# The second SwiGLU of each layer computed wholly in quads of seven products, with the output projection and the down projections reordered around its start

## The chip, the core and the metric

The kernel runs on one core of one Trainium2 chip. The metric is the device time of one execution in microseconds (us): 2252.36 us is the median of three runs of the kernel before (2252.14 to 2252.47).

The names of the engines are those of the profile: PE (matrix multiplication) with PEld (its weight loads), DVE (vector), ACT (scalar and activation), POOL and SP (here the queue that issues loads).

## The reference, cut to what matters

There are two layers (`DEPTH`), 512 positions (`SEQ`), a model width of 1024 and a hidden width of 2816 in each SwiGLU. A layer is

```
h = h + 0.5 * swiglu(rmsnorm(h, ffn1_norm), ffn1_w_gu, ffn1_w_down)
u = rmsnorm(h, mix_norm)                  # gated convolution and attention of u
h = h + merged @ w_o                      # output projection of the mixer
h = h + 0.5 * swiglu(rmsnorm(h, ffn2_norm), ffn2_w_gu, ffn2_w_down)
h = h + sigmoid(rmsnorm(h) @ w_pg) * (p @ w_pp)

swiglu(x): g, u = split(x @ w_gu);  return (silu(g) * u) @ w_down
```

The change concerns the line with `w_o` and the SwiGLU behind it, in both layers.

## The kernel before, in words

**Numbers in two parts.** The state `h` lies transposed in SBUF as eight tiles `h[0..7]` of 128 features by 512 positions. Every operand of a product is split into a rounded high part and a low part (`split`, `split_to`), and a product is the sum hi·hi + hi·lo + lo·hi, so three matrix multiplications (`mm3`, L266 to L270). Weights come from HBM as raw tiles `st` of 128x1024, which hold eight 128x128 blocks; ACT rounds a raw tile to `wh` (L71) and DVE subtracts to get `wl` (L72). There are four buffers each for `wh` and `wl` and ten for raw tiles, handed out in turn: the fifth split waits until PE has done with the first.

**A SwiGLU (`ffn`).** `normed` (L357) makes the split inputs `xs[k]` and the sum of squares of the eight `h[k]`; `rms` turns that sum into the factor `r`, which is applied behind the products. The 22 column blocks of the hidden width are computed in two ways. *Whole* blocks are plain projections: two column tiles (gate and up) times eight `xs`, 96 matrix multiplications of 512 columns for two blocks (`projs`, `proj`). *Quads* (`Sevens`, `Halved`) compute two blocks at once by seven products in place of eight: `Halved.row(j)` forms sums and differences of halves of `h[j]` and `h[j+4]` (`t`, `u`), and `Quad.part(j)` forms sums and differences of four raw weight tiles on DVE. Products 1, 2, 3, 4 and 6 are *joint*: eight wide multiplications of 512 columns (`wh` against high and low part together, L527) and eight narrow ones of 256 columns (`wl`, L533). Products 5 and 7 take 24 multiplications of 256 columns (L547). In `narrow_first` products the narrow ones come first.

**Accumulators of a quad.** Product 1 opens accumulator `b`; a copy of it by ACT (L552) opens `a`, which takes product 2; after product 6 another copy of `b` opens `d`, which takes 5 and 3; `b` goes on with 7 and 4. `Sevens.out` empties an accumulator: ACT copies one half (L556), DVE adds the other (L557), `finish` multiplies by `r`, applies silu and multiplies up with gate. PSUM holds two buffers for `b` (pool `bp`), one shared by `a` and `d` (pool `ap`), and two single banks (`mp`).

**Order.** The order on every engine comes from a scheduler that takes instructions by the order of the program and by its own estimate of when they are ready; `tc.issue_after(x)` adds that the instructions of the block that run on the engine of `x` stand behind `x` there. In `ffn`, all SwiGLUs but the very first begin with two whole blocks: `projs` of block 0 runs while DVE and ACT finish the norm and the rows, and the two projections of block 1 stand between the products of quad 1 (L727 to L741). From there on `next_quad` (L656) lays out every quad as product 1 of the next, product 4 of this one, a fill, 2, 6, a fill, 5, 7, 3, two fills. A *fill* (`fill`, L651) is a down projection `down(m, f0, f0+4)`: ACT writes 2·h[m] into a single bank (L640), 12 multiplications add four hidden blocks, and ACT writes half of the sum back to `h[m]` (L644).

**Output projection.** L1057 to L1060 compute `h[m] += w_o` block by block, m = 0 to 7.

Of the kernel before, what the change touches and what calls it, by code (L numbers as in the profile page):

```python
# [13 lines left out]
ALU = mybir.AluOpType  # L14
AX = mybir.AxisListType

P = 128
# [16 lines left out]
class Stream:  # L34
# [43 lines left out]
    def fill(self):  # L78
        return 0 if self.tiles is None else len(self.tiles) % 8
# [50 lines left out]
class Quad:  # L130


    def __init__(self, W, quarters):
        self.W = W
        for q in ("a11", "a21", "a22", "a12"):
            setattr(self, q, W.raw(quarters[q]))

    def part(self, j):

        W = self.W  # L140
        tt = W.nc.vector.tensor_tensor
        if j == 1:
# [16 lines left out]
        return W.split(self.a11)  # L159


class HiLo(tuple):
# [20 lines left out]
def trunk_kernel(ctx, tc, dims, x, p, positions, gains, rope_c, final_row, weights, out):  # L183
# [19 lines left out]
    class Banks:  # L203


        def __init__(self):
            self.scope, self.n = None, 0

        def close(self):
            if self.scope is not None:  # L210
                self.scope.close()
            self.scope = ExitStack()
            self.n += 1
# [8 lines left out]

        def paired(self):
            self.close()
            self.chain, self.seeded, self.single = self.pool("bp", 2), self.pool("ap", 1), self.pool("mp", 2)

    banks = Banks()
    ctx.callback(lambda: banks.scope.close())
# [4 lines left out]
    def two(pool, name):  # L233
        return pool.tile([P, 1024], F32, tag="bb", name=name).rearrange("p (w t) -> p w t", t=512)

    def PB(name):
        return two(banks.chain, name)

    def PA(name):
        return two(banks.seeded, name)  # L240

    def halves(t):
        return [t[:, 0, :], t[:, 1, :]]
# [9 lines left out]
    def split(src, name, scale=None, paired=False):  # L253
        v = X(name) if paired else (G(name + "h", F32R), G(name + "l", F32R))
        split_to(*v, src, scale)
        return v

    def split_to(hi, lo, src, scale=None):
        if scale is None:
            nc.scalar.copy(hi, src)  # L260
            return nc.vector.tensor_tensor(lo, src, hi.bitcast(F32), ALU.subtract)
# [54 lines left out]
    def gain(nm, l, k):  # L316
        c = col_at[nm, l] + k
        return cols[:, c:c + 1]
# [35 lines left out]
        nc.vector.scalar_tensor_tensor(r, t, 1.5 * scale, r, ALU.add, ALU.mult)  # L354
        return r

    def normed(nm, l, name, after=None, paired=True):  # L357

        xs, sq = [], Squares(name)
        for k in range(KD):  # L360
            xs.append(split(h[k], f"{name}x{k}", gain(nm, l, k), paired))
            sq.add(h[k])
            if after:
                after(k, xs)
        return xs, sq.parts()
# [81 lines left out]
    class Halved:  # L447
# [11 lines left out]
        def row(self, j, xs):  # L459

            self.own(j, xs)
            self.other(j, xs)

        def own(self, j, xs):

# [10 lines left out]
        def other(self, j, xs):  # L476

            H = S // 2
            left, right = slice(0, H), slice(H, S)
            k = j + KD // 2  # L480
            x, t, th, tl = self.half.pop(j)
            y, u = G(f"{self.name}y{j}"), G(f"{self.name}u{j}")
            nc.scalar.mul(y, h[k], gain(self.nm, self.l, k))
            nc.vector.tensor_tensor(t[:, right], y[:, right], x[:, right], ALU.subtract)
            nc.vector.tensor_tensor(u[:, left], t[:, right], x[:, left], ALU.add)
            nc.vector.tensor_tensor(u[:, right], y[:, left], u[:, left], ALU.subtract)
            split_to(th, tl, t)
            self.ys[7].append((th[:, right], tl[:, right]))
            for p_, at in ((2, left), (3, right)):
                self.ys[p_].append(self.both(xs[k], at))  # L490
            for p_, at in ((6, left), (4, right)):
                v = G(f"{self.name}u{j}_{p_}", F32R).rearrange("p (a t) -> p a t", t=H)
                split_to(v[:, 0, :], v[:, 1, :], u[:, at])
                self.ys[p_].append((v[:, 0, :], v))

    class Sevens:

# [6 lines left out]
        def __init__(self, w, l, name, ys, columns, done):  # L504
            self.w, self.l, self.name, self.ys, self.columns, self.done = w, l, name, ys, columns, done
            self.todo = {}
            self.narrow_first = ()

        def quad(self, n):
            if n not in self.todo:  # L510
# [9 lines left out]
        def joint(self, ps, d, j):  # L520

            hi, lo = d["w"].part(j)
            at = [slice(i * P, (i + 1) * P) for i in range(8)]
            def wide(last):
                for k, (_, pair) in enumerate(self.ys[j]):
                    for w in range(2):
                        nc.tensor.matmul(ps[:, w, :].rearrange("p (a t) -> p a t", t=self.H), hi[:, at[2 * k + w]], pair,  # L527
                                         start=j == 1 and k == 0, stop=last and k == 3, skip_group_check=True)

            def narrow(last):  # L530
                for k, (vh, _) in enumerate(self.ys[j]):
                    for w in range(2):
                        nc.tensor.matmul(ps[:, w, :self.H], lo[:, at[2 * k + w]], vh, start=False, stop=last and k == 3,  # L533
                                         skip_group_check=True)

            parts = (narrow, wide) if j in self.narrow_first else (wide, narrow)
            for i, part in enumerate(parts):
                part(i == 1)

        def product(self, ps, d, j):  # L540

# [6 lines left out]

        def seed(self, n, what):
            d = self.todo[n]  # L550
            d[what] = PA(f"{self.name}{n}{what}")
            nc.scalar.copy(d[what].rearrange("p w t -> p (w t)"), d["b"].rearrange("p w t -> p (w t)"))  # L552

        def out(self, n, ps, f, c):
            t = self.tile(n, f"o{f}{c}")
            nc.scalar.copy(t, ps[:, :, self.H:])  # L556
            nc.vector.tensor_tensor(t, ps[:, :, :self.H], t, ALU.add)  # L557
            self.done(n, f, c, t, t)

        def step(self, n, j):  # L560
            d, H = self.quad(n), self.H
# [23 lines left out]
                self.joint(d["b"], d, j)  # L585
                self.out(n, d.pop("b"), 1, 0)

    def ffn(l, nm, name, first=False, beside=iter(()), early=2):
# [26 lines left out]
        if not first:  # L615
            sevens.narrow_first = (3, 4, 6)

        def early_rows(k, xs):

            if 0 <= k - KD // 2 < early:  # L620
                ys.row(k - KD // 2, xs)

        xs, acc = normed(nm, l, name, early_rows)

        pss, pds = {}, {}

# [23 lines left out]

        def fill():  # L651
            if downs:
                m, f0 = downs.pop(0)
                down(m, f0, f0 + 4)

        def next_quad(n):  # L656

            for i, j in enumerate((1, 4, None, 2, 6, None, 5, 7, 3, None, None)):
                next(beside, None)
                if j is None:  # L660
                    if i < 9 or downs and downs[0][1] < f_last:
                        fill()
                    continue
                step(n if j == 4 else n + 1, j)
                if j == 6 and n % 2:
                    downs.extend((m, 2 * n - 2) for m in range(KD))

        cs = [[W.col(nm + "_w_gu", l, c + f * P, D) for c in (0, DFF)] for f in range(n_whole)]

# [7 lines left out]
        if first:  # L677
# [23 lines left out]
            downs.extend((m, 0) for m in range(KD))  # L701
            fill()
            with tc.issue_after(second):
                step(n0, 5)
# [1 line left out]
                step(n0, 3)  # L706
            sevens.narrow_first = (3, 4, 6)
            for _ in range(2):
                fill()
        else:  # L710
            pss[0] = whole(0)
# [12 lines left out]
            step(n0, 7)  # L724
            step(n0, 3)
        fill()
        for n in range(n0, np_ - 1):  # L727
            next_quad(n)

        f0 = f_last  # L730
        left = [m for m in range(KD) if (m, f0) in downs]
        assert len(left) == len(downs)
        spare = PA(f"{name}pd")[:, 0, :]
        for m in left[:3]:
# [23 lines left out]
    def mixer(l):  # L758
# [498 lines left out]
    for l in range(DEPTH):  # L1257
        ffn(l, "ffn1", f"a{l}", l == 0, rotary() if l == 0 else iter(()), 2 if l else 0)
        mixer(l)
        ffn(l, "ffn2", f"b{l}")  # L1260
        (ple_last if l == DEPTH - 1 else ple)(l)

    return W.halves
# [46 lines left out]
```

## Time and profile before

| | us |
|---|---|
| median of three runs | 2252.36 |
| the profiled execution's own time | 2252.33 |
| its span, first to last instruction | 2250.3 |
| PE busy in it | 2240.8 |
| DVE busy | 1743.5 |
| ACT busy | 1456.1 |
| POOL busy | 37.4 |

Busy time of PE counts overlapping multiplications once, and their ends are modelled, so what a stretch costs is read from the starts of its multiplications. The granted PE clock over the span is 0.999. In the first layer the output projection ends and the second SwiGLU begins at 729.15 us; tiles of that SwiGLU carry the prefix `b0`, those of the second layer `b1`.

### The profile page before, as it was taken

Reading aid. Unit: us, or ns where it says so; the run is one execution under the profiler, and the core shown is the slowest. Engines: PE = TensorE matmul, PEld = TensorE weight load, DVE = VectorE, ACT = ScalarE, POOL = GpSimd, SP = SyncE. Lnnn points to the kernel's source line nnn. Section 1 sums busy time; section 2 is a strip of 40 time slices with the busy share of each in tenths; the row PEclk is TensorE's granted clock in tenths of the full one; section 3 lists DMA queues with packets and bytes.
Section 4 is the critical chain, followed back from the end, with each engine's and each line's share of the span. In section 5 each row is a group of like instructions: output and inputs, shape, how many; then the busy total and the mean of one; then the engine's idle time right before and its main releaser. Section 6 shows DMA issues by size and latency. Waiting matters only on the chain.

```text
span 2250.3 us, 31142 instructions
## 1 busy us (share of the span) xinstructions
PE 2240.8 (100%) x12144; PEld 1947.7 (87%) x12144; DVE 1743.5 (77%) x2453; ACT 1456.1 (65%) x2246; POOL 37.4 (2%) x42
## 2 busy tenths in 40 slices
PE   9999999999999999999999999999999999999998
PEld 8888888888888888888888888888888888888887
DVE  8987768788866887776798777687889678777756
ACT  7666666576744666667676666764767357666664
POOL 0000000000200000000000000000001000000000
PEclk9999999999999999999999999999999999999999
DMA  5333332323132232334223233323222223333321
GB/s 215 99 113 104 103 122 75 112 76 104 47 104 84 94 103 97 107 107 141 75 94 104 96 106 108 113 88 102 92 76 75 94 75 103 104 104 103 108 99 38
DMA packets 63362, 223.04 MB, mean 99 GB/s; under 512 B 7280, under 2 KB 7280, under 8 KB 63216
## 3 DMA queue, kind: packets, MB, share of 16 engines
q1 hardware_dynamic: 62640, 220.28, 29.2%
q8 instruction: 95, 1.56, 0.3%
q10 hardware_dynamic: 576, 0.79, 0.1%
q14 instruction: 51, 0.42, 0.1%
HBM read 218.94 MB, written 2.10 MB: 98 GB/s over the span
## 4 chain that ended last, share of the span: by engine, by line
PE 97%; DVE 2%; ACT 1%; issue 0%; DVEq 0%
PE a0pd L268 2%; PE a1pd L268 2%; PE b0pd L268 2%; PE b1pd L268 2%; PE a0pd L269 2%; PE a0pd L270 2%; PE b1pd L269 2%; PE b0pd L269 2%; PE a1pd L269 2%; PE b1pd L270 2%; PE b0pd L270 2%; PE a1pd L270 2%; PE m0mop L268 1%; PE m1mop L269 1%; PE m0mop L269 1%; PE m1mop L270 1%
## 5 line engine op out<-in xcount | busy, mean ns | idle before, releaser
L72 DVE TENSOR_TENSOR wl<-st,wh 128x1024 fp32r<-128x1024 f32 (+1 forms) x508 | 614.7, 1212 | 227.5 <-ACT wh L71 224.1
L71 ACT CAST wh<-st 128x1024 fp32r<-128x1024 f32 (+1 forms) x507 | 527.9, 1044 | 306.6 <-PE m1Bp L269 13.9
L71 ACT CAST wh<-s 128x1024 fp32r<-128x1024 f32 x49 | 51.6, 1052 | 28.8 <-PE m1Cp L269 4.2
L72 DVE TENSOR_TENSOR wl<-s,wh 128x1024 fp32r<-128x1024 f32 x49 | 59.6, 1216 | 0.3 <-ACT wh L71 0.3
L152 DVE TENSOR_TENSOR st<-st,st 128x1024 f32<-128x1024 f32 x49 | 59.7, 1219 | 0.2
L154 DVE TENSOR_TENSOR s<-st,st 128x1024 f32<-128x1024 f32 x49 | 59.6, 1217 | 0.1
L149 DVE TENSOR_TENSOR st<-st,s 128x1024 f32<-128x1024 f32 x49 | 59.6, 1216 | 0.0
L157 DVE TENSOR_TENSOR st<-st,st 128x1024 f32<-128x1024 f32 x49 | 59.6, 1216 | 0.0
L644 ACT ACTIVATE h<-a0pd 128x512 f32<-128x512 f32 x40 | 23.7, 594 | 5.6 <-PE a0pd L270 5.3
L644 ACT ACTIVATE h<-b1pd 128x512 f32<-128x512 f32 x40 | 23.7, 592 | 4.9 <-PE b1pd L270 4.8
L644 ACT ACTIVATE h<-b0pd 128x512 f32<-128x512 f32 x40 | 23.7, 592 | 4.7 <-PE b0pd L270 4.6
L644 ACT ACTIVATE h<-a1pd 128x512 f32<-128x512 f32 x40 | 23.6, 591 | 4.5 <-PE a1pd L270 4.4
L640 ACT ACTIVATE a1pd<-h 128x512 f32<-128x512 f32 x40 | 24.0, 599 | 0.7
L640 ACT ACTIVATE b1pd<-h 128x512 f32<-128x512 f32 x40 | 23.9, 599 | 0.6
L640 ACT ACTIVATE b0pd<-h 128x512 f32<-128x512 f32 x40 | 23.9, 598 | 0.6
L640 ACT ACTIVATE a0pd<-h 128x512 f32<-128x512 f32 x40 | 23.9, 598 | 0.6
L107 POOL MEMSET wh<- 128x256 f32 x4 | 1.1, 314 | 1173.3 <-DVE wl L72 1173.3
L268 PE MATMUL a0p<-a0x,wh 128*128 128x512 f32 x44 | 17.1, 390 | 0.0
L269 PE MATMUL a0p<-a0x,wh 128*128 128x512 f32 x44 | 17.1, 390 | 0.0
L270 PE MATMUL a0p<-a0x,wl 128*128 128x512 f32 x44 | 17.1, 389 | 0.0
L263 ACT ACTIVATE b0x<-h,cols 128x512 fp32r<-128x512 f32 x8 | 5.8, 724 | 13.3 <-DVE h L1060 13.3
L263 ACT ACTIVATE b1x<-h,cols 128x512 fp32r<-128x512 f32 x8 | 5.8, 723 | 13.3 <-DVE h L1060 13.3
(6945 smaller groups left out, 7503.9 us busy)
## 6 DMA issues: line engine op xcount, KB each, us to landing
st<-in_weights SPq DMA_DIRECT2D x406, 512.0 KB, 3.3
h<-in_x SPq DMA_DIRECT2D x8, 256.0 KB, 5.4
st<-in_weights SPq DMA_DIRECT2D x7, 256.0 KB, 5.3
out<-e1d SPq DMA_DIRECT2D x4, 256.0 KB, 2.1
out<-fh SPq DMA_DIRECT2D x3, 256.0 KB, 2.2
e0pi<-in_p SPq DMA_DIRECT2D x2, 256.0 KB, 3.5
e1pi<-in_p SPq DMA_DIRECT2D x2, 256.0 KB, 3.8
fg<-in_final_row SPq DMA_DIRECT2D x2, 256.0 KB, 4.5
```

What stands on the lines that cost most here:

```text
L71: self.nc.scalar.copy(hi[:, w], src[:, w])
L72: self.nc.vector.tensor_tensor(lo[:, w], src[:, w], hi[:, w].bitcast(F32), ALU.subtract)
L149: tt(self.a12, self.a12, self.s, ALU.subtract)
L152: tt(self.a11, self.a11, self.a21, ALU.subtract)
L154: tt(self.s, self.a22, self.a11, ALU.subtract)
L157: tt(self.a21, self.a21, self.a22, ALU.add)
L263: nc.scalar.activation(hi, src, AF.Copy, scale=scale)
L268: nc.tensor.matmul(ps, wh, vh, start=first, stop=False, skip_group_check=seeded)
L269: nc.tensor.matmul(ps, wh, vl, start=False, stop=False, skip_group_check=seeded)
L270: return nc.tensor.matmul(ps, wl, vh, start=False, stop=last, skip_group_check=seeded)
L640: nc.scalar.mul(ps, h[m], 2.0)
L644: nc.scalar.mul(h[m], ps, 0.5)
```

## The change

In both second SwiGLUs (`quads=True`) there are no whole blocks left: the 22 hidden blocks are eleven quads, 0 to 10.

- The output projection computes blocks 0 and 4 together, k by k, in the two banks of the `ap` buffer, and then 1, 5, 2, 6, 3, 7; the norm follows that order. `own(j)` and `other(j)` of the rows are called as soon as `h[j]` and `h[j+4]` exist, so all four rows stand ahead of the first product.
- `Quad.early` splits parts 1 and 2 of quad 0 into ordinary 128x512 buffers and forms all sums of that quad's weights while the output projection runs.
- Product 1 of quad 1 and product 2 of quad 0 are computed in two parts: 1 of quad 0, wide part of 1 of quad 1, wide part of 2 of quad 0, 6 of quad 0, narrow part of 2, narrow part of 1; then 5, 7, 3, 4 of quad 0, 2 and 6 of quad 1, 1 of quad 2, and 5, 7, 3 of quad 1. The accumulator `d` of quad 0 has a PSUM buffer of its own (`PX`), which becomes the two single banks afterwards.
- The down projections start behind product 3 of quad 1, with blocks 0 and 1 alone for all m; blocks 2 and 3 follow, then four at a time. So each `h[m]` goes to PSUM and back once more. `fill` takes two of the short ones at a time, and also two where it meets `(0, f0, 4)`: in the first SwiGLUs of both layers the fills thus run one ahead.

```diff
+    def early(self, split):                                   # class Quad
+        tt = self.W.nc.vector.tensor_tensor
+        self.ready[1] = split(self.a11)
+        self.ready[2] = split(self.a12)
+        tt(self.a11, self.a11, self.a21, ALU.subtract)
+        self.s = self.W.buffer("s")
+        tt(self.s, self.a22, self.a11, ALU.subtract)
+        tt(self.a12, self.a12, self.s, ALU.subtract)
+        tt(self.a21, self.a21, self.a22, ALU.add)
...
+        def rest(self, kind, name, bufs):                     # class Banks
+            if getattr(self, "part", None) is not None:
+                self.part.close()
+            whole, self.scope = self.scope, ExitStack()
+            setattr(self, kind, self.pool(name, bufs))
+            self.part, self.scope = self.scope, whole
+        def singles_to_spare(self):
+            self.rest("spare", "xp", 1)
+        def spare_to_singles(self):
+            self.rest("single", "mp", 2)
...
+        def opened(self, n):                                  # class Sevens
+            d = self.quad(n)
+            d["b"] = PB(f"{self.name}{n}b")
+            return self.joint(d["b"], d, 1, True)
+        def second(self, n):
+            d = self.quad(n)
+            return self.joint(d["a"], d, 2, True)
...
-        n_whole = 4 if first else 2
+        n_whole = 4 if first else 0 if quads else 2
...
         def fill():
             if downs:
-                m, f0 = downs.pop(0)
-                down(m, f0, f0 + 4)
+                m, f0, f1 = downs.pop(0)
+                down(m, f0, f1)
+                if (f1 == 2 or f1 == 4 and m == 0) and downs:
+                    m, f0, f1 = downs.pop(0)
+                    down(m, f0, f1)
...
+        elif quads:
+            sevens.where[0, "d"] = PX
+            last_row, last_act = ends
+            banks.singles_to_spare()
+            with tc.issue_after(proj.last.ins):
+                step(0, 1)
+            wide_1, narrow_1 = sevens.opened(1)
+            with tc.issue_after(sevens.last):
+                after = wide_1()
+            r = rms(acc, D, name, ps=halves(PX(name + "ps"))[0])
+            wide_2, narrow_2 = sevens.second(0)
+            with tc.issue_after(after):
+                after = wide_2()
+            with tc.issue_after(after):
+                step(0, 6)
+            with tc.issue_after(sevens.last):
+                narrow_2()
+                sevens.second_out(0)
+                after = narrow_1()
+            with tc.issue_after(last_row), tc.issue_after(last_act), tc.issue_after(after):
+                step(0, 5)
+                step(0, 7)
+                step(0, 3)
+                banks.spare_to_singles()
+                sevens.seed(1, "a")
+                step(0, 4)
+                step(1, 2)
+                step(1, 6)
+            with tc.issue_after(sevens.last):
+                for part in sevens.opened(2):
+                    after = part()
+            with tc.issue_after(after):
+                for j in (5, 7, 3):
+                    step(1, j)
+            sevens.seed(2, "a")
+            downs.extend((m, 0, 2) for m in range(KD))
+            with tc.issue_after(sevens.last):
+                fill()
...
-        for m in range(KD):
-            ps = proj(W.col("w_o", l, m * P, D), merged, f"{name}wop{m}")
+        m0, m1 = halfway[:2]
+        two_ps = halves(PA(f"{name}wop"))
+        projs([W.col("w_o", l, m * P, D) for m in (m0, m1)], merged, two_ps)
+        for i, m in enumerate(halfway):
+            ps = two_ps[i] if i < 2 else proj(W.col("w_o", l, m * P, D), merged, f"{name}wop{m}")
             nc.vector.tensor_tensor(h[m], ps, h[m], ALU.add)
```

**Where the order moves.** The names read out<-in; `b01d` is accumulator `d` of quad 1 in SwiGLU `b0`. First ACT, before: the stretch in which `d` of the first quad (there quad 1) is opened (L552).

```order
L260 CAST b0a0h<-b0un_7024 128x512
L556 COPY b01o_7115<-b01a 128x512
L71 CAST wh_7253<-st_7039 128x1024
L552 COPY b01d<-b01b 128x1024
L604 ACTIVATE b01o_7115<-b01o_7115 128x256
```

On PE a whole projection, `b0pu`, stands between product 6 (into `b01b`) and product 5 (into `b01d`) there. Now the same place on ACT for quad 0 (L607 opens an accumulator, L611 empties one, L400 to L402 are the norm's factor):

```order
L310 CAST b0ah<-b0acc 128x512
L71 CAST wh_7087<-st_6821 128x1024
L71 CAST wh_7117<-st_6819 128x1024
L400 ACT_TABLE_LOAD
L400 ACTIVATE b0r<-b0ps,eps_t 128x512
L71 CAST wh_7150<-st_6825 128x1024
L401 ACTIVATE b0t<-b0r 128x512
L402 ACTIVATE b0ms<-b0ps,eps_t 128x512
L611 COPY b00o_7072<-b00a 128x512
L607 COPY b00d<-b00b 128x1024
```

The copy that opens `b00d` now stands behind the norm, three weight splits and the emptying of `b00a`; on PE it is the two narrow parts that lie between product 6 and product 5.

Second, PE, before: product 3 of quad 1 ends, product 1 of quad 2 (`b02b`) follows, then product 4 of quad 1.

```order
L527 MATMUL b01d<-b0x_6901,wh_7253 128x512 x2
L527 MATMUL b02b<-b0x_6820,wh_7292 128x512 x2
L527 MATMUL b02b<-b0x_6825,wh_7292 128x512 x2
L527 MATMUL b02b<-b0x_6831,wh_7292 128x512 x2
L527 MATMUL b02b<-b0x_6837,wh_7292 128x512 x2
L533 MATMUL b02b<-b0x_6820,wl_7293 128x256 x2
L533 MATMUL b02b<-b0x_6825,wl_7293 128x256 x2
L533 MATMUL b02b<-b0x_6831,wl_7293 128x256 x2
L533 MATMUL b02b<-b0x_6837,wl_7293 128x256 x2
L533 MATMUL b01b<-b0u_4_6866,wl_7315 128x256 x2
```

Now product 1 of quad 2 stands between product 6 of quad 1 (`b01b`) and product 5 of quad 1 (`b01d`), with no fill beside it:

```order
L578 MATMUL b01b<-b0u_6_6969,wh_7246 128x512 x2
L578 MATMUL b02b<-b0x_6848,wh_7277 128x512 x2
L578 MATMUL b02b<-b0x_6879,wh_7277 128x512 x2
L578 MATMUL b02b<-b0x_6911,wh_7277 128x512 x2
L578 MATMUL b02b<-b0x_6943,wh_7277 128x512 x2
L585 MATMUL b02b<-b0x_6848,wl_7278 128x256 x2
L585 MATMUL b02b<-b0x_6879,wl_7278 128x256 x2
L585 MATMUL b02b<-b0x_6911,wl_7278 128x256 x2
L585 MATMUL b02b<-b0x_6943,wl_7278 128x256 x2
L602 MATMUL b01d<-b0t0h,wh_7298 128x256
```

Third, ACT and DVE at that same place, now. ACT splits part 3 of quad 1 (`wh_7362`), empties `b00b`, splits the first down-projection tile (`wh_7398`), empties `b01a` and opens `b01d`:

```order
L71 CAST wh_7362<-st_7008 128x1024
L611 COPY b00o_7206<-b00b 128x512
L673 ACTIVATE b00o_7206<-b00o_7206 128x256
L71 CAST wh_7398<-st_7396 128x1024
L310 CAST b0a1h<-b0an_7148 128x512
L611 COPY b01o_7236<-b01a 128x512
L607 COPY b01d<-b01b 128x1024
```

DVE has the other halves of the same steps (L612 is the add that empties an accumulator):

```order
L72 TENSOR_TENSOR wl_7363<-st_7008,wh_7362 128x1024
L612 TENSOR_TENSOR b00o_7206<-b00b,b00o_7206 128x512
L175 TENSOR_TENSOR st_7270<-st_7270,st_7272 128x1024
L672 TENSOR_TENSOR b00o_7206<-b00o_7206,b0r 128x512
L677 TENSOR_TENSOR b0an_7148<-b00o_7206 128x256
L72 TENSOR_TENSOR wl_7399<-st_7396,wh_7398 128x1024
L311 TENSOR_TENSOR b0a1l<-b0an_7148,b0a1h 128x512
L612 TENSOR_TENSOR b01o_7236<-b01a,b01o_7236 128x512
```

What moved: `b02b` reuses the buffer of `b00b`, which this order empties behind `wh_7362` and `wl_7363`; `b01d` reuses that of `b01a`, which is emptied behind `wh_7398` and `wl_7399`. `wh_7362` reuses the buffer of product 6 of quad 1 (`wh_7246`), `wh_7398` and `wl_7399` those of product 1 of quad 2 (`wh_7277`, `wl_7278`). The rows of the second layer (`b1`) are the same.

More of the change, by code (lines that the diff above doesn't have):

```diff
@@ L141, in part @@
         tt = W.nc.vector.tensor_tensor
+        if j in self.ready:
+            return self.ready.pop(j)
+        if self.summed:
+            return W.split({3: self.a12, 4: self.a22, 5: self.a21, 6: self.s, 7: self.a11}[j])
         if j == 1:
@@ L159, in part, with __init__, __getitem__ @@
         return W.split(self.a11)
+class Pieces:
+    def __init__(self, tiles):
+        self.tiles = tiles
+    def __getitem__(self, key):
+        rows, c = key
+        i, start = divmod(c.start, 512)
+        return self.tiles[i][rows, start:start + c.stop - c.start]
 class HiLo(tuple):
@@ L240, in PA, with PX @@
         return two(banks.seeded, name)
+    def PX(name):
+        return two(banks.spare, name)
     def halves(t):
@@ L355, in rms, with normed @@
         return r
[L357 to L361, printed above, removed]
+    def normed(nm, l, name, after=None, paired=True, order=range(8)):
+        xs, sq = [None] * KD, Squares(name)
+        for k in order:
+            xs[k] = split(h[k], f"{name}x{k}", gain(nm, l, k), paired)
             sq.add(h[k])
@@ L461, in row @@
             self.own(j, xs)
-            self.other(j, xs)
+            return self.other(j, xs)
         def own(self, j, xs):
@@ L506, in __init__ @@
             self.todo = {}
-            self.narrow_first = ()
+            self.narrow_first, self.where = (), {}
         def quad(self, n):
@@ L526, in wide @@
                     for w in range(2):
-                        nc.tensor.matmul(ps[:, w, :].rearrange("p (a t) -> p a t", t=self.H), hi[:, at[2 * k + w]], pair,
-                                         start=j == 1 and k == 0, stop=last and k == 3, skip_group_check=True)
+                        end = nc.tensor.matmul(ps[:, w, :].rearrange("p (a t) -> p a t", t=self.H), hi[:, at[2 * k + w]], pair,
+                                               start=j == 1 and k == 0, stop=last and k == 3, skip_group_check=True)
+                return end.ins
             def narrow(last):
@@ L532, in narrow @@
                     for w in range(2):
-                        nc.tensor.matmul(ps[:, w, :self.H], lo[:, at[2 * k + w]], vh, start=False, stop=last and k == 3,
-                                         skip_group_check=True)
+                        end = nc.tensor.matmul(ps[:, w, :self.H], lo[:, at[2 * k + w]], vh, start=False, stop=last and k == 3,
+                                               skip_group_check=True)
+                return end.ins
             parts = (narrow, wide) if j in self.narrow_first else (wide, narrow)
+            if apart:
+                return [lambda last=i == 1, part=part: part(last) for i, part in enumerate(parts)]
             for i, part in enumerate(parts):
-                part(i == 1)
+                self.last = part(i == 1)
         def product(self, ps, d, j):
@@ L586, in step, with ffn @@
                 self.out(n, d.pop("b"), 1, 0)
-    def ffn(l, nm, name, first=False, beside=iter(()), early=2):
+    halfway = (0, 4, 1, 5, 2, 6, 3, 7)
+    def ffn(l, nm, name, first=False, beside=iter(()), early=2, quads=False):
         H = S // 2
@@ L616, in ffn, with pieces @@
             sevens.narrow_first = (3, 4, 6)
+        ends = []
         def early_rows(k, xs):
-            if 0 <= k - KD // 2 < early:
-                ys.row(k - KD // 2, xs)
-        xs, acc = normed(nm, l, name, early_rows)
+            j = k - KD // 2
+            if quads:
+                ends[:] = [ys.own(k, xs) if j < 0 else ys.other(j, xs), split_to.hi]
+            elif 0 <= j < early:
+                ys.row(j, xs)
+        if quads:
+            def pieces(src):
+                parts = [split(src[:, c:c + 512], f"{name}q{c}") for c in (0, 512)]
+                return Pieces([a for a, _ in parts]), Pieces([b for _, b in parts])
+            sevens.quad(0)["w"].early(pieces)
+        xs, acc = normed(nm, l, name, early_rows, order=halfway if quads else range(KD))
         pss, pds = {}, {}
@@ L663, in next_quad @@
                     continue
-                step(n if j == 4 else n + 1, j)
+                if n > 1 or j != 1 or not quads:
+                    step(n if j == 4 else n + 1, j)
                 if j == 6 and n % 2:
-                    downs.extend((m, 2 * n - 2) for m in range(KD))
+                    downs.extend((m, max(2 * n - 2, 2 if quads and n else 0), 2 * n + 2) for m in range(KD))
         cs = [[W.col(nm + "_w_gu", l, c + f * P, D) for c in (0, DFF)] for f in range(n_whole)]
@@ L700, in ffn @@
             activate(3)
-            downs.extend((m, 0) for m in range(KD))
+            downs.extend((m, 0, 4) for m in range(KD))
             fill()
@@ L726, in ffn @@
         fill()
-        for n in range(n0, np_ - 1):
+        for n in range(1 if quads else n0, np_ - 1):
             next_quad(n)
         f0 = f_last
-        left = [m for m in range(KD) if (m, f0) in downs]
+        left = [m for m in range(KD) if (m, f0, f0 + 4) in downs]
         assert len(left) == len(downs)
```

21 lines of the change are left out of this document (15 added, 6 removed).

## The prediction

> **What bounds the kernel now.** I read the page first: busy times, then the shares of the chain that ended last.
>
> ```profile
> span 2250.3 us, 31142 instructions
> PE 2240.8 (100%) x12144; PEld 1947.7 (87%) x12144; DVE 1743.5 (77%) x2453; ACT 1456.1 (65%) x2246; POOL 37.4 (2%) x42
> ...
> PE 97%; DVE 2%; ACT 1%; issue 0%; DVEq 0%
> ```
>
> PE is busy for all but 9.5 us of the span, and 97% of the chain is PE. The waits of PE say whether anything holds it up.
>
> ```profile
> PE idle L376 <- DVE hpi L305: 1.0, 1, 1.0
> PE m0cop L270 <- DVE wl L72: 0.3, 1, 0.3
> PE m1cop L270 <- DVE wl L72: 0.3, 1, 0.3
> ```
>
> That is all: 1.0 us ahead of the first multiplication and twice 0.3 us in the mixers. So PE is gap-free in the stretch that changes, and time can be gained only by taking multiplications out, while each new wait of PE is lost in full. DVE and ACT have slack on average; what counts is where it lies. The timeline of PE around quad 1 gives its paces:
>
> ```profile
> 748.76 1.98 PE L527 MATMUL b01a<-b0x,wh 128*128 128x512 f32 x8
> 750.57 1.11 PE L533 MATMUL b01a<-b0x,wl 128*128 128x256 f32 x8
> 751.52 1.12 PE L533 MATMUL b01b<-b0u,wl 128*128 128x256 f32 x8
> 752.48 2.00 PE L527 MATMUL b01b<-b0u,wh 128*128 128x512 f32 x8
> 754.32 0.39 PE L268 MATMUL b0pu<-b0x,wh 128*128 128x512 f32 x1
> ...
> 759.76 0.28 PE L547 MATMUL b01d<-b0t0h,wh 128*128 128x256 f32 x1
> ```
>
> From start to start, eight wide multiplications take 1.81 us (748.76 to 750.57) and eight narrow ones 0.95, so a joint product takes 2.77. The 24 of `b0pu` take 759.76 - 754.32 = 5.44 us, or 0.2267 each. Note where they stand: between the last multiplication into `b01b` and the first into `b01d`. The chain gives the price of a product 5 or 7:
>
> ```profile
> 95.17 2.87 PE a03d L547 x24
> ```
>
> That is 0.120 for each multiplication of 256 columns.
>
> **The gain.** In each second SwiGLU 96 multiplications of 512 columns (two whole blocks) become one more quad: five joint products with 40 of 512 and 40 of 256, and two products of 24 of 256. So 56 x 0.2267 = 12.69 us go and 88 x 0.120 = 10.54 come: 2.15 us for one SwiGLU, 4.3 for both. That is 0.19%, just under the 0.2% (4.5 us) that a measurement of this kernel can tell from no change. The Trainium skill ("TensorE: Matmul & The Clock Gate", section "Back-to-back issue gap") gives N / 2.4 + 2.5 ns for one multiplication; by that the gain would be 56 x 0.2158 - 88 x 0.1092 = 2.48 us, 4.96 for both, just over the bound. The rows above are longer, and I go by them.
>
> **What the whole projections covered.** Taking them out also takes out the 5.44 us between products 6 and 5 of the first quad. Rows of ACT and DVE there:
>
> ```profile
> 741.20 1.28 ACT L350 ACT_TABLE_LOAD   x1
> 742.49 0.69 ACT L350 ACTIVATE b0r<-b0ps,eps_t 128x512 f32<-128x512 f32 x1
> 743.08 0.71 ACT L483 ACTIVATE b0y<-h,cols 128x512 f32<-128x512 f32 x1
> 743.69 0.62 ACT L351 ACTIVATE b0t<-b0r 128x512 f32<-128x512 f32 x1
> 744.21 0.68 ACT L352 ACTIVATE b0ms<-b0ps,eps_t 128x512 f32<-128x512 f32 x1
> 744.78 0.62 ACT L260 CAST b0t3h<-b0t 128x512 fp32r<-128x512 f32 x1
> 745.29 1.02 ACT L552 COPY b01a<-b01b 128x1024 f32<-128x1024 f32 x1
> 746.23 0.71 ACT L260 CAST b0u<-b0u 128x256 fp32r<-128x256 f32 x2
> 746.84 1.06 ACT L71 CAST wh<-s 128x1024 fp32r<-128x1024 f32 x1
> 747.79 1.05 ACT L71 CAST wh<-st 128x1024 fp32r<-128x1024 f32 x1
> ...
> 752.59 0.62 ACT L260 CAST b0a0h<-b0un 128x512 fp32r<-128x512 f32 x1
> 753.11 0.58 ACT L556 COPY b01o<-b01a 128x512 f32<-128x512 f32 x1
> 754.58 1.05 ACT L71 CAST wh<-st 128x1024 fp32r<-128x1024 f32 x1 [0.89 <-PE b01b L527]
> 755.54 1.00 ACT L552 COPY b01d<-b01b 128x1024 f32<-128x1024 f32 x1
> ```
>
> ```profile
> 751.77 2.36 DVE L72 TENSOR_TENSOR wl<-st,wh 128x1024 fp32r<-128x1024 f32 x2
> 754.05 0.68 DVE L261 TENSOR_TENSOR b0a0l<-b0un,b0a0h 128x512 fp32r<-128x512 f32 x1
> 754.65 0.68 DVE L557 TENSOR_TENSOR b01o<-b01a,b01o 128x512 f32<-128x512 f32 x1
> ...
> 757.12 0.42 DVE L608 TENSOR_TENSOR b0an<-b01o 128x256 f32<-128x256 f32 x1
> ```
>
> `b01d` was opened from 755.54 to 756.54, over 2 us behind product 6 (ended 754.32), and nobody noticed, since PE had `b0pu` until 759.76. Without such cover each step counts. From these rows: a release by PE reaches ACT after 0.26 us (754.32 to 754.58). A split of 1024 takes ACT 1.05, or 0.95 where work follows; the subtraction takes DVE 1.14; 512 columns take DVE 0.60, or 0.68 if someone waits for the end; the copy that opens an accumulator takes 1.00. I put 0.05 for a hop between ACT and DVE, as a guess. With them I walk through the new order, which is the same in both layers; the semaphores fix who waits for whom.
>
> First, the norm and small waits. The two sums into `b0ps` wait for the split of `b0acc`, behind four casts of ACT: about 0.3 us. Later two short fills follow each other in two single banks, and a third waits for the write-back (about 0.6 on ACT), half of it covered: 0.3. I take 0.6 in all; bounds 0 and 1.5.
>
> Second, `b00d`, counted from the start of product 1 of quad 0. PE gets there after 2.77 + 1.81 + (1.81 + 2 x 0.227) + 0.3 + 2.77 + 0.95 + 0.95 = 11.8 us. ACT starts on `b00a` at 2.77 + 0.26 = 3.0 and then has, by the rows' pitches, 0.94 (that copy), 0.52, 0.61 and 0.52 (casts), 1.90 (two weight splits), 1.28 (table), 0.59 (`r`), 0.95 (a split), 0.52, 0.57 (`t`, `ms`) and 0.52 (emptying `b00a`): at 11.9 it starts to open `b00d` and ends at 12.9 to 13.0. PE waits 1.2 us. Were ACT wholly free, emptying `b00a` could start 0.26 behind narrow part 2 (10.85) and PE would still wait 0.8; upper bound 1.6.
>
> Third, `b02b`, directly behind product 6 of quad 1. It needs the buffer of `b00b`, which PE left two products (5.5 us) earlier, but DVE empties it behind `wl_7363`, which needs `wh_7362`, and that cast waits for the end of product 6 itself: 0.26 + 1.05 + 0.05 + 1.14 + 0.68 + 0.05 = 3.2 us of waiting. Bounds 3.0 and 3.4.
>
> Fourth, `b01d`, directly behind `b02b`. `wh_7398` starts when the wide half of `b02b` is done, so it ends about 0.4 behind the narrow half; then come `wl_7399` 1.14, `b0a1l` 0.60, the emptying of `b01a` 0.68, the opening by ACT 1.00, hops 0.1: 3.9 us. Bounds 3.6 and 4.2.
>
> Both long waits stand although the buffers' old contents were finished long before: the wait is behind other instructions in the queues, and who queues behind `wh_7362` and `wl_7363` is just what PE needs next.
>
> Sum for one SwiGLU: 0.6 + 1.2 + 3.2 + 3.9 = 8.9 lost, 2.15 gained, net 6.75; for both 13.5.
>
> **Edits at no cost.** `early` adds some 4 us on ACT and 7 on DVE during the output projection, whose eight blocks are 8 x 5.44 = 43.5 us of PE; if that cover were gone it would cost up to 4. Blocks 0 and 4 together use each merged tile half as fast: 0. Sixteen more pairs of copies between `h` and PSUM (0.6 each) lie beside products. The loads stand in the same order of use: 0. In the first SwiGLUs a fill moves one place ahead and leaves one gap in the cover of a product, whose accumulators have 2.77 us: 0, at most 1 for both.
>
> **The clock.** A pause of PE may cost more than itself. The windows at the end of the run, PE's last multiplication ahead of them:
>
> ```profile
> 2242.09 0.28 PE L1123 MATMUL e1pg<-kh,e1x 128*128 128x256 f32 x1
> ```
>
> ```profile
> 2243.00:2244.00 1.00, 0.00 (x0) 0.00 (x0) 0.96 (x6) 1.00 (x1) 0.00 (x0) 1.00 0.69 256
> 2244.00:2245.00 1.00, 0.00 (x0) 0.00 (x0) 0.93 (x4) 0.54 (x3) 0.00 (x0) 0.81 0.07 23
> 2245.00:2246.00 1.00, 0.00 (x0) 0.00 (x0) 0.78 (x5) 0.39 (x2) 0.00 (x0) 0.50 0.00 0
> ```
>
> PEclk (third number from the right) is 1.00, 0.81, 0.50: it fell to half at 2244.62, 2.25 us after PE ended at 2242.37. The third and fourth waits are longer than that, the second isn't. What the return costs is seen only at the run's start, against the same form later:
>
> ```profile
> 1.03 3.78 PE L376 MATMUL idle<-ones 128*128 128x128 f32 x16 [1.03 <-DVE hpi L305]
> 4.61 1.46 PE L377 MATMUL idle<-ones 128*128 128x512 f32 x2
> 602.76 1.25 PE L989 MATMUL m0t11t<-ident,m0s11e 128*128 128x128 f32 x10
> 603.77 0.36 PE L970 MATMUL m0s21p<-m0h2kn1h,m0h2qn1h 128*128 128x256 f32 x1
> ```
>
> Sixteen take 3.58 us, 0.224 each, against 0.101 later: 2.0 us lost until the pace is full (though PEclk doesn't show it there). One sighting of the fall can't say that every pause over 2.25 us has one, so I take three of the four long waits: 3 x 2.0 = 6.0 us; bounds none and four (8.0).
>
> 2252.3 + 13.5 + 6.0 = 2271.8, so **2272 us**. The profiled execution's own 2252.33 equals the median of 2252.36 within 0.03, so nothing is added.
>
> **Rivals.** *The clock holds* over pauses below 4 us: then 2252.3 + 13.5 = 2266 us. For it: one sighting, at the end of a run, may be a matter of phase. Against it: that sighting. The Trainium skill (same page, section "What's actually happening") has the clock fall after at least one idle window of about 3.4 us; by that 3.2 us never holds a window and 3.9 only where it is aligned, and the time is this rival's. The fall after 2.25 us above speaks against a full window.
>
> *DVE falls behind* through the quads that now come before the fills. Until the fills start DVE has in a quad eleven weight operations (seven subtractions, four sums) at 1.14, four outputs at 0.60 + 0.60 + 0.42 (emptied, times `r`, times gate) and two more adds of 0.60: 12.5 + 6.5 + 1.2 = 20.2 us, against 5 x 2.77 + 2 x 2.87 = 19.6 of PE. If the delay isn't caught up, the pair of long waits comes back once more at the next quad, 3.2 + 3.9 less the 0.6 of small waits, 6.5 us for each SwiGLU: 2272 + 13 = 2285 us. Against it: fills of 12 x 0.2267 = 2.72 us follow, which ask little of DVE, and the long waits themselves give DVE time.
>
> *The other side: the long waits don't arise.* Place: `wh_7362`. If its buffer were free one product earlier than I read, the cast would run during product 2 of quad 1, `b00b` would be empty 2 us before PE comes, and `wh_7398` would move ahead likewise; the change then does what it says. The gain comes through with the small waits hidden: 2252.3 - 4.3 = 2248 us. It decides at whether that cast starts before product 6 of quad 1 ends. Against it: four buffers for `wh` in turn, and the cast at 754.58, which waited for exactly such a release.
>
> **How the numbers follow.** Forecast 0.55, clock holds 0.28, DVE behind 0.09, other side 0.08. The range covers the first two with the bounds: 0.8 + 3.0 + 3.6 lost without falls, net 5.25, gives 2252.3 + 10.5 = 2262.8; 1.5 + 1.6 + 3.4 + 4.2, net 8.55, with four falls gives 2252.3 + 17.1 + 8.0 = 2277.4: 2262 to 2278. Slower by over 0.2% is 0.92; the other side is mostly within 0.2% (0.06), faster 0.02.
>
> **What would show it.** In the changed profile's waits of PE: `b02b` and `b01d` (in the second layer `b12b`, `b11d`) with about 3.2 and 3.9 us, released by DVE L612 and ACT L607, `b00d` with 1.2; 112 x 0.2267 us of multiplications gone and 176 x 0.120 come; PEclk about 0.8 in the window behind the long waits. I am wrong if `wh_7362` starts before product 6 ends, if PE busy falls by 4.3 with no new waits, or if PE waits in quads 2 and 3 as well.

## The result, and the profile after

| | before | changed |
|---|---|---|
| median, us (four runs each, on one chip) | 2252.41 (2252.14 to 2252.60) | 2275.45 (2274.65 to 2276.58) |
| span of the profiled execution | 2250.3 | 2273.4 |
| PE busy | 2240.8 | 2248.1 |
| mean granted PE clock | 0.999 | 0.994 |

The changed kernel is slower by 23.0 us: ratio 1.0102, 95% interval 1.0090 to 1.0115. The forecast was 2272 us in a range of 2262 to 2278.

The page of the changed kernel, at the places that were read before:

```profile
span 2273.4 us, 31383 instructions
PE 2248.1 (99%) x12208; PEld 1953.8 (86%) x12208; DVE 1765.2 (78%) x2483; ACT 1482.6 (65%) x2304; POOL 37.3 (2%) x42
...
PE 95%; DVE 3%; ACT 2%; issue 0%; DVEq 0%
```

PE has 64 multiplications more (176 narrow ones come, 112 wide ones go), as counted. It is busy for longer although its multiplications should take 4.3 us less; that is a first hint of a lower clock. Its waits (columns: us in total, times, longest):

```profile
PE b01d L602 <- ACT b01d L607: 3.7, 1, 3.7
PE b11d L602 <- ACT b11d L607: 3.6, 1, 3.6
PE b12b L578 <- DVE b10o L612: 3.1, 1, 3.1
PE b02b L578 <- DVE b00o L612: 3.1, 1, 3.1
PE b00d L602 <- ACT b00d L607: 1.0, 1, 1.0
...
PE b10d L602 <- ACT b10d L607: 1.0, 1, 1.0
```

Three waits in each second SwiGLU, with the tiles, releasers and sizes that the walk through the new order gave (3.9, 3.2 and 1.2). The lost time lies in these two SwiGLUs. From its first multiplication to its last one, the second SwiGLU of the first layer took 1068.09 - 729.15 = 338.94 us before, and now takes 1079.55 - 729.23 = 350.32. These are the two ends before,

```profile
729.15 0.39 PE L268 MATMUL b0p<-b0x,wh 128*128 128x512 f32 x1
...
1068.09 0.39 PE L270 MATMUL b0pd<-b0a21h,wl 128*128 128x512 f32 x1
```

and these after:

```profile
729.23 1.07 PE L578 MATMUL b00b<-b0x,b0q0h 128*128 128x512 f32 x4
...
1079.55 0.39 PE L320 MATMUL b0pd<-b0a21h,wl 128*128 128x512 f32 x1
```

That is 11.4 us in the first layer; the other 11.7 lie in the second one. The timeline of PE shows both long pauses (the bracket is the idle time ahead and what ended it):

```profile
758.81 0.61 PE L578 MATMUL b01b<-b0u,wh 128*128 128x512 f32 x2
762.53 3.48 PE L578 MATMUL b02b<-b0x,wh 128*128 128x512 f32 x8 [3.11 <-DVE b00o L612]
765.85 1.11 PE L585 MATMUL b02b<-b0x,wl 128*128 128x256 f32 x8
770.64 0.58 PE L602 MATMUL b01d<-b0t0h,wh 128*128 128x256 f32 x1 [3.69 <-ACT b01d L607]
771.02 0.42 PE L602 MATMUL b01d<-b0t0l,wh 128*128 128x256 f32 x1
```

Counted from start to start, as the sum does, the first costs 762.53 - 758.81 - 2 x 0.227 = 3.27 us and the second 770.64 - 765.85 - 8 x 0.120 = 3.83. And the multiplications behind each pause are slow: the eight wide ones of `b02b` take 765.85 - 762.53 = 3.32 us in place of 1.81, and the narrow ones of `b01d` stand 0.21 us apart in place of 0.12. ACT and DVE in that stretch of the changed kernel:

```profile
759.47 1.04 ACT L71 CAST wh<-st 128x1024 fp32r<-128x1024 f32 x1
760.42 0.58 ACT L611 COPY b00o<-b00b 128x512 f32<-128x512 f32 x1
...
766.05 1.05 ACT L71 CAST wh<-st 128x1024 fp32r<-128x1024 f32 x1 [1.48 <-PE b02b L578]
...
767.52 0.58 ACT L611 COPY b01o<-b01a 128x512 f32<-128x512 f32 x1
769.59 1.00 ACT L607 COPY b01d<-b01b 128x1024 f32<-128x1024 f32 x1 [1.50 <-DVE b01o L612]
```

```profile
760.57 1.21 DVE L72 TENSOR_TENSOR wl<-st,wh 128x1024 fp32r<-128x1024 f32 x1
761.71 0.68 DVE L612 TENSOR_TENSOR b00o<-b00b,b00o 128x512 f32<-128x512 f32 x1
...
767.13 1.23 DVE L72 TENSOR_TENSOR wl<-st,wh 128x1024 fp32r<-128x1024 f32 x1 [2.11 <-ACT wh L71]
...
768.88 0.68 DVE L612 TENSOR_TENSOR b01o<-b01a,b01o 128x512 f32<-128x512 f32 x1
```

The reader sees the two chains one below the other. Product 6 of quad 1 ends at about 759.3; the cast of part 3 starts at 759.47, its subtraction on DVE at 760.57, and only then DVE empties `b00b` (761.71 to 762.39); `b02b` starts at 762.53. In the same way the cast and subtraction for the first down projections stand ahead of emptying `b01a` (768.88) and of opening `b01d` (769.59 to 770.59); PE starts at 770.64.

The windows of the changed kernel give the clock (PEclk is the third number from the right):

```profile
762.00:763.00 1.00, 0.47 (x1) 0.50 (x2) 1.00 (x2) 0.00 (x0) 0.00 (x0) 0.57 0.45 66
765.00:766.00 1.00, 1.00 (x6) 0.81 (x5) 0.03 (x1) 0.00 (x0) 0.00 (x0) 0.72 0.00 0
768.00:769.00 1.00, 0.00 (x0) 0.00 (x0) 1.00 (x3) 0.10 (x1) 0.00 (x0) 0.98 0.00 0
775.00:776.00 1.00, 1.00 (x8) 1.00 (x6) 0.00 (x0) 0.04 (x1) 0.00 (x0) 0.60 0.00 0
1888.00:1889.00 1.00, 0.70 (x2) 0.63 (x3) 1.00 (x2) 0.00 (x0) 0.00 (x0) 0.77 0.50 74
1891.00:1892.00 1.00, 1.00 (x4) 0.81 (x4) 0.00 (x0) 0.12 (x1) 0.00 (x0) 0.52 0.00 0
1895.00:1896.00 1.00, 0.00 (x0) 0.00 (x0) 0.97 (x2) 0.55 (x1) 0.00 (x0) 0.68 0.79 209
1902.00:1903.00 1.00, 1.00 (x9) 1.00 (x9) 0.11 (x1) 1.00 (x2) 0.00 (x0) 0.90 0.00 0
```

A mean of 0.57 in a window in which the clock goes from 1 to 0.5 puts the step at 762.14, and so on: down at 762.14, up at 765.56, down at 768.96, up at 775.80; in the second layer down at 1888.54, up at 1891.96, down at 1895.36, up at 1902.20. So each of the four long pauses had its fall. What a fall costs is read from the starts behind it. At PEclk 0.50 multiplications of 512 columns start 0.427 us apart (0.227 at 1.00) and those of 256 columns 0.213 (0.120), so somewhat less than half of the slow time is lost. In the first layer the wide ones of `b02b` take 3.32 - 1.81 = 1.51 us longer, and the 24 of `b01d`, from 770.64 to 775.88, 5.24 - 2.88 = 2.36. In the second layer, where PE restarted at 1888.30 and 1896.50, the multiplications behind the pauses take 1.67 and 2.58 us longer. Together that is 8.1 us; the kernel with filled pauses below shows that 0.1 us behind each pause is lost at full clock too, so about 7.7 us are the clock's.

### The profile page after: what moved, and what is told of

It reads as the page before. It is cut to its first block, busy times and chain, and to the rows that moved or that the text cites. A ratio compares the mean times of both kernels' runs of the same rounds, so it can differ in the third digit from the quotient of the medians.

```text
span 2273.4 us, 31383 instructions
## 1 busy us (share of the span) xinstructions
PE 2248.1 (99%) x12208; PEld 1953.8 (86%) x12208; DVE 1765.2 (78%) x2483; ACT 1482.6 (65%) x2304; POOL 37.3 (2%) x42
## 4 chain that ended last, share of the span: by engine, by line
PE 95%; DVE 3%; ACT 2%; issue 0%; DMA 0%; SPq 0%; DVEq 0%
PE b1pd L318 2%; PE b0pd L318 2%; PE a0pd L318 2%; PE a1pd L318 2%; PE b1pd L319 2%; PE b0pd L319 2%; PE a0pd L319 2%; PE b0pd L320 2%; PE a1pd L319 2%; PE a0pd L320 2%; PE b1pd L320 2%; PE a1pd L320 2%; DVE wl L72 1%; PE m1mop L318 1%; PE m0mop L318 1%; PE m0mop L320 1%
## 5 line engine op out<-in xcount | busy, mean ns | idle before, releaser
L724 ACT ACTIVATE h<-b1pd 128x512 f32<-128x512 f32 x48 | 28.3, 593 | 5.5 <-PE b1pd L320 5.2
L720 ACT ACTIVATE b1pd<-h 128x512 f32<-128x512 f32 x48 | 28.5, 601 | 0.6
L720 ACT ACTIVATE b0pd<-h 128x512 f32<-128x512 f32 x48 | 28.5, 600 | 0.6
L1246 PE MATMUL e1pg<-kh,e1x 128*128 128x512 f32 (+1 forms) x40 | 14.0, 349 | 0.0
```

What stands on the lines that cost most here:

```text
L720: nc.scalar.mul(ps, h[m], 2.0)
L724: nc.scalar.mul(h[m], ps, 0.5)
```

## The experiments

The theory: what costs the time is the order in which ACT and DVE take their work. The buffers that PE needs next are emptied behind weight splits that wait for PE itself, and each long pause then lowers the clock. The rivals: DVE, which the trace shows busy from 749.3 to 764.1 us but for one gap of 0.2, has too much to do there, whatever the order; the fall of the clock costs nothing beyond the pauses; some of the 23 us come from the smaller parts of the change. The first four experiments ran on one chip, where the kernel before took 2252.71 us (median of 27).

**The smaller parts alone.** The kernel before, with the fills of the first SwiGLUs one ahead and two output blocks interleaved:

```diff
-                m, f0 = downs.pop(0)
-                down(m, f0, f0 + 4)
+                for _ in range(2 if name[0] == "a" and downs[0] == (0, 0) else 1):
+                    m, f0 = downs.pop(0); down(m, f0, f0 + 4)
...
+        two_ps = projs([W.col("w_o", l, m * P, D) for m in (0, 1)], merged, halves(PA(f"{name}wop")))
         for m in range(KD):
-            ps = proj(W.col("w_o", l, m * P, D), merged, f"{name}wop{m}")
+            ps = two_ps[m] if m < 2 else proj(W.col("w_o", l, m * P, D), merged, f"{name}wop{m}")
```

> The kernel before with two smaller parts of the change alone: in the first SwiGLUs the first fill takes two down projections, and the first two blocks of the output projection (here 0 and 1) are computed k by k together. Theory (the cost of the change lies in the four long waits of the second SwiGLUs and in the clock behind them): these parts cost nothing, 2252.4 us, within 0.5. Rival (1 to 2 us of the changed kernel's 23 come from these parts): 2253.5 to 2254.5 us.

Measured: 2252.71 us (10 runs), ratio 1.0000 (0.9991 to 1.0009), and no wait of PE that the kernel before didn't have. These parts cost nothing.

**Pauses filled with idle multiplications.**

```diff
+            idle = PS(f"{name}idle"); a, b = xs[0]
             with tc.issue_after(sevens.last):
-                for part in sevens.opened(2):
-                    after = part()
+                w = [nc.tensor.matmul(idle, a[:, :P], a, start=True, stop=True) for _ in range(12)][-1].ins
+            with tc.issue_after(w):
+                for part in sevens.opened(2): after = part()
             with tc.issue_after(after):
+                w = [nc.tensor.matmul(idle, a[:, :P], a, start=True, stop=True) for _ in range(14)][-1].ins
+            with tc.issue_after(w):
                 for j in (5, 7, 3):
```

> The changed kernel with idle multiplications put into the two long waits of each second SwiGLU: 12 of 512 columns (2.72 us) ahead of product 1 of quad 2, 14 (3.17 us) ahead of product 5 of quad 1; their result is read by nobody. Theory (the waits end at the same time, but the granted clock no longer falls): PE's waits shrink to about 0.5 and 0.7 us, PEclk is 1.00 throughout, and 8.1 us come back: 2267.3 us, 2266.5 to 2268.5. Rival (the clock's fall costs nothing beyond the waits): 2275 us as before.

Measured: 2268.06 us (2267.89 to 2268.47), ratio 1.0069 (1.0054 to 1.0084); the mean granted clock is 0.999, and the waits are these:

```profile
PE b01d L602 <- ACT b01d L607: 0.5, 1, 0.5
PE b11d L602 <- ACT b11d L607: 0.5, 1, 0.5
PE b12b L578 <- DVE b10o L612: 0.4, 1, 0.4
PE b02b L578 <- DVE b00o L612: 0.4, 1, 0.4
```

Nothing useful was added and nothing was released earlier, yet the span is 2273.4 - 2265.7 = 7.7 us shorter than the changed kernel's. So about a third of the loss is the clock and not the pauses. At full clock the eight wide multiplications of `b02b` take 1.91 us and the 24 of `b01d` 2.97, still 0.1 more than without a pause ahead of them.

**The same instructions in another order.** Multiplying by `r`, silu and gate (`finish`) of three accumulators is issued behind product 6 of quad 1, so that emptying comes first:

```diff
-            self.done(n, f, c, t, t)
+            self.done(n, f, c, t, t) if self.held is None else self.held.append((n, f, c, t, t))
...
-                step(0, 5)
-                step(0, 7)
+                step(0, 5); step(0, 7); sevens.held = []
                 step(0, 3)
                 banks.spare_to_singles()
                 sevens.seed(1, "a")
                 step(0, 4)
                 step(1, 2)
                 step(1, 6)
+                held, sevens.held = sevens.held, None; [finish(*x) for x in held]
```

> The changed kernel with the same instructions in another order: the multiplications by r, silu and gate of three accumulators (03 and 04 of quad 0, 02 of quad 1) are issued behind product 6 of quad 1, so that the copies and adds that empty the buffers of b00b and b01a come ahead of them and of the weight splits. Theory (the buffers were empty late because of what stood ahead in the queues of ACT and DVE): both long waits go and the clock stays up, 2 x (3.28 + 3.84 + 3.85) = 21.9 us come back: 2253.5 us, 2252.5 to 2256. Rival (DVE, busy without a gap from 749.3 to 764.1 us, has too much to do there, whatever the order): the waits move to later products, less than half comes back, 2264 to 2272 us.

Measured: 2252.97 us (2252.70 to 2253.39), ratio 1.0002 (0.9993 to 1.0011). DVE in this kernel:

```profile
756.05 0.68 DVE L612 TENSOR_TENSOR b00o<-b00b,b00o 128x512 f32<-128x512 f32 x1
...
757.85 1.22 DVE L72 TENSOR_TENSOR wl<-st,wh 128x1024 fp32r<-128x1024 f32 x1
758.98 0.69 DVE L612 TENSOR_TENSOR b01o<-b01a,b01o 128x512 f32<-128x512 f32 x1
```

and PE:

```profile
759.68 1.98 PE L578 MATMUL b02b<-b0x,wh 128*128 128x512 f32 x8
761.50 1.12 PE L585 MATMUL b02b<-b0x,wl 128*128 128x256 f32 x8
762.45 0.28 PE L602 MATMUL b01d<-b0t0h,wh 128*128 128x256 f32 x1
```

`b00b` is empty at 756.73, 3 us ahead of `b02b` at 759.68, where it was emptied at 762.39 in the changed kernel; PE runs from `b02b` into `b01d` without a pause. DVE has the same work, but both of its adds of 512 that empty the buffers (756.05 and 758.98) now come ahead of the cast of ACT that waits for product 6, and of the subtraction behind that cast:

```profile
759.88 1.06 ACT L71 CAST wh<-st 128x1024 fp32r<-128x1024 f32 x1 [0.52 <-PE b01b L578]
```

The order was the cause, and DVE's load wasn't.

**The third wait removed too.** On ACT the copy that opens `b00d` also goes ahead of emptying `b00a` and of the split of part 3:

```diff
-            nc.scalar.copy(d[what].rearrange("p w t -> p (w t)"), d["b"].rearrange("p w t -> p (w t)"))
+            self.seeded = nc.scalar.copy(d[what].rearrange("p w t -> p (w t)"), d["b"].rearrange("p w t -> p (w t)")).ins
...
-                step(0, 6)
-            with tc.issue_after(sevens.last):
+                step(0, 6); seeded = sevens.seeded
+            with tc.issue_after(sevens.last), tc.issue_after(seeded):
...
-                step(0, 3)
+                with tc.issue_after(seeded): step(0, 3)
```

> As the kernel with the later multiplications by r, and the copy that opens b00d also goes ahead of the split of part 3 of quad 0 and of the emptying of b00a on ACT. Theory: the wait of 1.2 us at product 5 of quad 0 goes as well, and the gain of 2.15 us in each second SwiGLU comes through but for some tenths: 2251 us, 2249 to 2252; faster than the kernel before by 0.3 to 3 us. Rival (DVE has too much to do): 2262 to 2270 us.

(The kernel meant by "the later multiplications by r" is the one just above.) Measured: 2251.04 us, eleven runs of 2250.77 to 2251.82, against 2251.97 to 2253.20 for the 27 runs of the kernel before. The two don't overlap, but the ratio of 0.9993 has an interval of 0.9985 to 1.0002, so a gain of 1.7 us is likely and not certain. The second SwiGLU of the first layer takes 1068.08 - 729.98 = 338.10 us here,

```profile
729.98 0.61 PE L578 MATMUL b00b<-b0x,b0q0h 128*128 128x512 f32 x2
...
1068.08 0.39 PE L320 MATMUL b0pd<-b0a21h,wl 128*128 128x512 f32 x1
```

0.84 less than before, where 2.15 were to be had. The other 1.3 us lie in small waits, here the third short down projection, which takes the bank of the first one:

```profile
772.68 0.39 PE L320 MATMUL b0pd<-b0a1h,wl 128*128 128x512 f32 x1
773.04 0.50 PE L318 MATMUL b0pd<-b0a0h,wh 128*128 128x512 f32 x1
773.37 0.39 PE L319 MATMUL b0pd<-b0a0l,wh 128*128 128x512 f32 x1
```

The starts are 0.36 and 0.33 apart in place of 0.227: 0.24 us. About as much goes at the two sums of the norm and 0.3 once more among the fills; the rest are pieces of about 0.1. They were not taken out.

**Shorter pauses.** The kernel with idle multiplications, with fewer of them, and other numbers in each layer (`l`). This is the first kernel; the second has `(6, 10)[l]` and `(9, 5)[l]`:

```diff
-                w = [nc.tensor.matmul(idle, a[:, :P], a, start=True, stop=True) for _ in range(12)][-1].ins
+                w = [nc.tensor.matmul(idle, a[:, :P], a, start=True, stop=True) for _ in range((4, 8)[l])][-1].ins
...
-                w = [nc.tensor.matmul(idle, a[:, :P], a, start=True, stop=True) for _ in range(14)][-1].ins
+                w = [nc.tensor.matmul(idle, a[:, :P], a, start=True, stop=True) for _ in range((7, 10)[l])][-1].ins
```

> The changed kernel with fewer idle multiplications in its long waits: 4 and 7 in the first layer, 8 and 10 in the second, so that PE pauses for about 2.3, 2.2, 1.4 and 1.5 us. Theory (the clock is judged at the ends of windows of 3.413 us, the step between its changes in the changed kernel's records, and falls where PE was busy for less than about half of a window): the pauses of 1.4 and 1.5 us leave 56% of any window busy, and the clock holds in the second layer; the pauses of 2.2 and 2.3 us fall only where one window holds at least 1.7 us of one. 2267 to 2271 us. Rival (a fall 2.25 us after PE stops, as the forecast had it): none in the second layer, and at most one at the very end of a pause in the first. Rival by the Trainium skill (TensorE: Matmul & The Clock Gate, section What's actually happening: at least one idle window of about 3.4 us): none in either layer, 2268 us.

> The same with 6 and 9 idle multiplications in the first layer, 10 and 5 in the second, so that PE pauses for about 1.8, 1.7, 0.9 and 2.6 us. Theory (windows of 3.413 us, a fall where PE was busy for less than about half of one): the clock holds at 0.9 us; at 1.7 and 1.8 us it falls only if nearly all of the pause lies in one window; at 2.6 us it falls if one window holds 1.7 us of it, so in about half of the phases or more. Rival (2.25 us after PE stops): a fall at 2.6 us alone, about 0.3 us ahead of the end of the pause. Rival by the Trainium skill (same place): none.

Measured, one run each beside 2252.75 us of the kernel before: 2268.60 us for the first, whose pauses of 2.2, 2.1, 1.3 and 1.6 us had no fall (mean granted clock 0.999); 2272.49 us for the second, whose pauses of 1.8, 1.6, 0.9 and 3.0 us had two, at the first and the last. Windows and PE of the second at its first pause:

```profile
764.00:765.00 1.00, 1.00 (x6) 0.82 (x5) 1.00 (x2) 0.00 (x0) 0.00 (x0) 0.95 0.93 377
765.00:766.00 1.00, 1.00 (x5) 0.81 (x4) 0.43 (x2) 0.47 (x2) 0.00 (x0) 0.50 0.14 53
...
768.00:769.00 1.00, 1.00 (x6) 0.77 (x5) 1.00 (x2) 0.00 (x0) 0.00 (x0) 0.85 0.00 0
```

```profile
761.01 0.61 PE L824 MATMUL b0idle<-b0x 128*128 128x512 f32 x2
763.42 0.93 PE L578 MATMUL b02b<-b0x,wh 128*128 128x512 f32 x3 [1.79 <-DVE b00o L612]
```

PE stood from 761.62 to 763.42, and the clock fell at 764.90, 1.5 us after PE was running again, and rose at 768.30. That rules out both rivals, which the first kernel couldn't tell from the theory: PE had stopped for less than 2.25 us, and no window of 3.4 us was wholly idle. It fits windows of 3.413 us: the one from 761.49 to 764.90 was idle for 1.80 us, 53%, and the clock fell. The second pause (1.60 us, in the window from 768.31 to 771.72) took 47% of one, and the clock held.

The first kernel tells more when its windows are laid back from the one change at its end. These are PE at its first pause and the window of that change:

```profile
759.49 1.07 PE L824 MATMUL b0idle<-b0x 128*128 128x512 f32 x4
762.80 2.08 PE L578 MATMUL b02b<-b0x,wh 128*128 128x512 f32 x8 [2.25 <-DVE b00o L612]
```

```profile
2262.00:2263.00 1.00, 0.00 (x0) 0.00 (x0) 0.64 (x1) 0.60 (x1) 0.00 (x0) 0.92 0.00 0
```

The clock fell at 2262.84; 439 steps of 3.4133 us (the length worked out in the last section) ahead of it is 764.38. So the window from 760.97 to 764.38 was idle until 762.80, for 1.83 us or 54%, and the clock held, though the expectation put the bound at about half of a window, 1.7 us. Its second pause, idle for 1.72 us of a window (50%), held as well. So the windows are borne out, but the share at which the clock falls was put a little too low: by the ends shown 1.83 us held where 1.80 fell in the second kernel. The ends of multiplications are modelled, and that can be the difference: counted by starts, the last idle multiplication of the second kernel was done at 761.01 + 2 x 0.227 = 761.46, so its window from 761.49 on was idle for 1.93 us, 57%.

## Why the prediction was right, and where its sizes were off

| term, both SwiGLUs | forecast, us | measured, us |
|---|---|---|
| multiplications saved | -4.3 | -4.3 (by count) |
| norm and short fills | 1.2 | 3.1 (what is left over) |
| `b00d`, `b10d` | 2.4 | 2.4 |
| `b02b`, `b12b` | 6.4 | 6.5 |
| `b01d`, `b11d` | 7.8 | 7.6 |
| clock | 6.0 | 7.7 |
| sum | 19.5 | 23.0 |

*The walk through the order* held at every wait: tile, releaser and size. That the emptying stood behind the splits, and that this and no lack of time was the cause, is shown by the kernel in another order.

*The whole projections as cover* held. They were 5.44 us between products 6 and 5; with them gone, what ACT and DVE do there must come early by order.

*The gain* is there but doesn't come through whole: the best order keeps 0.84 of 2.15 us in the first layer's SwiGLU.

*The clock* was right in kind and too small: the step "three of the four long waits, 2.0 us each". All four fell. The price was between 1.4 and 2.5 us, 1.9 in the mean, so that 2.0 came out right for all four together, though it was taken from the start of the run, a different case: that is partly luck. What failed is the reading of the one sighting as a delay of 2.25 us behind the last multiplication. The clock is judged by windows whose phase has nothing to do with the pause; so it may fall sooner, and the return takes one or two windows. The sighting fits that too: the window that ended with the fall at 2244.62 was idle for its last 2.25 us, 66%. The free phase would also explain why the four runs of the changed kernel spread over 1.9 us and the four with filled pauses over 0.6 (argued, not tried by itself).

*The small waits* were forecast at 0.6 us for each SwiGLU and come to about 1.5; this term is as far off as the clock. The norm's share was right (0.24 against 0.3), and 0.2 is the slow starts behind the two long pauses; the fills wait at more places than the one that was named. The rest was not measured piece by piece.

*The edits at no cost* cost nothing: two of them were run without the rest of the change, and with all of them the second SwiGLU of the first layer starts at 729.23 us in place of 729.15. *DVE behind* didn't happen: no wait of PE in quads 2 and 3 is as long as 0.3 us. *The other side* needed the cast of part 3 to start before product 6 ended; it started at 759.47, behind it.

## What to carry to other kernels

When work is taken out of a full engine, ask first what that work was covering: follow the next buffer that the engine needs back to the instruction that empties it, and look at what stands ahead of that instruction in its own queue. Here 4.3 us of saved multiplications cost 27 us of waits and slow clock, and issuing a few instructions later brought 22.5 of them back. A pause of an engine can cost more than its length; compare the pace behind it with the pace ahead of it.

## What the runs showed of the hardware

The granted clock of PE changes in steps of a fixed grid. In the changed kernel it changed at 762.14, 765.56, 768.96 and 775.80 in the first layer; four steps are 13.66 us there, 3.415 each. By that, 1888.54 in the second layer lies 330 steps behind 762.14, and 1126.40 / 330 gives 3.4133 us for a step.

At full clock, each long pause of the changed kernel filled between 59% and 91% of the window ahead of the change, and all four fell; windows with PE idle for 47% and 50% (both kernels with shorter pauses) held. Between them the modelled ends can't decide: 53% fell in one run and 54% held in another. So little more than half of a window is enough, and the exact share stays open.

At half clock, the window from 768.96 to 772.39 was half idle (PE restarted at 770.64) and the one from 1895.36 to 1898.78 a third (1896.50); both were followed by a second slow window, so the return took 6.84 us; a window that was idle for 0.39 us (762.14 to 762.53) was enough for the return. The Trainium skill ("TensorE: Matmul & The Clock Gate", section "What's actually happening") gives windows of about 3.4 us, which the steps agree with, but a fall only after at least one idle window; by the runs little more than half of one is enough.
